# A hybrid decoder step: streams for block inverses and decode, norm and gate in two halves, shift state read first, one tile per feature block

## The chip, the cores and the metric

The kernel runs on one core of one Trainium2 chip. TensorE multiplies matrices, VectorE (DVE in the profile), ScalarE (ACT) and GpSimd (POOL) work on tiles, SyncE (SP) issues most transfers. The metric is the device time of one execution in microseconds (us); of several runs, the median.

## The reference

One inference step of two layers for 1040 prompt tokens (16 of them meta tokens) and 8 decode sequences of one token each, 1024 features, all in float32. Layer 0 is a Conformer convolution, layer 1 an RWKV-7 time mixing, each followed by an MLP with squared ReLU (1024 to 4096 to 1024). What matters here is the time mixing and what follows it:

```
xx = prev - h                      # prev: the row before; for decode, state_shift
r, k, v = (h + xx*mix_r) @ w_r, (h + xx*mix_k) @ w_k, (h + xx*mix_v) @ w_v
decay, a, g = small two-step projections of h + xx*mix
per token and head:  S = S*w + (S @ -kk) (kk*a)^T + v k^T ;  y = S r
y   = groupnorm_per_head(y) * gn_g + gn_b
out = (y + (sum r*k*r_k) * v) * g @ w_o
h   = h + out ;  h = h + relu(rmsnorm(h) @ w_in)^2 @ w_out ;  final rmsnorm
```

Outputs are the normalised rows, and the new convolution, shift and matrix states.

## The kernel before

**Stages.** Layer 0 runs over three token groups of about 350 (`G0`). Then the mixing stage runs over four groups of about 264 tokens (`G1`, `mixer_in(0)` to `mixer_in(3)`), and the last stage, the output projection and the second MLP, over three groups (`G2`): group 0 alone, then groups 1 and 2 together. Products of weights and activations in layer 0, in the output projection and in the MLPs are made of three passes: weights and activations are split into a high and a low part (`split`, `load_w`), and `mm3` (L185) multiplies high by high, low by high and high by low. The projections r, k, v of the mixing stage use one float32 product (`proj`).

**The recurrence in chunks.** The state update is done in 17 chunks of 64 tokens (chunk 0 holds the 16 meta tokens). A chunk needs the inverse of small triangular blocks of 32. `inverses(c, n)` (L1116) reads n chunks' blocks from DRAM (`ni`), does 30 steps of one multiplication and one addition on VectorE (L1127, L1128), and writes the result to DRAM (`d_p`). `front(c)` (L1142) loads a chunk's operands, multiplies them (`A`, L1168), and turns the inverse into `x32`; `chunk(c)` then computes gg, W, po, U, S and Y. In the kernel before, `front` begins with the inverses: for chunk 0 alone, and at chunks 1, 5, 9 and 13 for four chunks. They can begin once the mixing group that makes the blocks has run its `tail`, which is placed behind the two small projections (`p_g`, `p_wa`) of the next group.

**Order.** Within `tc.manual_schedule` TensorE executes in the order in which the program issues; that holds for the mixing stage, and for the output projection and MLP of group 0. The order on the other engines, and on TensorE elsewhere, is chosen by a planner from modelled times. The recurrence, the norm and gate and the decode step are Python generators that are advanced at marked points. In the mixing stage the point is `tick` (L1412): it adds 2.0 credits to the recurrence (none in group 0), which spends them by the numbers that it yields (`RW`, together 27.72 per chunk), and takes one step of norm and gate. A group has a tick before each r projection and two within each projection, 56 in groups 1 and 2, 40 in group 3. `step(c + 1)` takes one step of the next chunk's front without a charge, three times per chunk. In the MLP the point is `fill` (208 of them for group 0), and `filler` (L285) advances each stream in proportion to a total (`FA`, `NGA`).

**Norm and gate.** `norm_gate(i)` (L1362) handles 128 tokens in two halves of 512 features: it loads y, takes mean and variance per head, normalises, transposes on TensorE (`yn`, L1388), scales on ScalarE, adds the bonus `bv` and multiplies by the gate `gt`, and stores to `d_z`. Its steps follow each other. The square `sq` and the gated result `z` use one buffer (tag `eq`).

**Decode.** `decode_step` (L1320) updates the eight states on VectorE in 16 pieces. It comes first in the stream that then does norm and gate, and uses that stream's buffers (`ey`, `eq`).

**Other lines of the change.** `prepare(g)` (L781) loads a group's rows and makes `xx`; in the last group it also reads the shift state, transposes it, and writes the new one. `narrow_w` (L908) loads the first weights of the small projections in two halves. `mlp_in` (L263) makes the MLP's activations `m_h`, `m_l` and, first, the sum of squares by ones on TensorE (`st_m`, L231), whose result `rs` is needed only behind the first product (`r`, L327). `mixer_out` (L1443) loads z block by block (`zr`), splits it (`z_h`, `z_l`) and multiplies by the output weights (`ps_oo`). Memory comes from pools that are opened one behind the other; a tile of a new pool waits until the tile that lay there is done with.

Of the kernel before, what the change touches and what calls it, by code (L numbers as in the profile page):

```python
# [16 lines left out]
P = 128  # L17
# [31 lines left out]
def hybrid_step(tc, x_prompt, x_sample, state_conv, state_shift, state_wkv, meta_tokens,  # L49
# [10 lines left out]
    with ctx:  # L60
# [133 lines left out]
        def dense(w, act, n, name, fill=None):  # L194
            ps = bank(f"ps_{name}")
            for k in range(KT):
                mm3(ps[:, :n], (w[0][:, k, :], w[1][:, k, :]), (act[0][:, k, :n], act[1][:, k, :n]), k == 0, k == KT - 1)
                if fill and k == KT // 2 - 1:
                    fill()
            return ps  # L200

# [61 lines left out]
        def mlp_in(pl, hv, n, layer, name, sums):  # L263

            rs = rstd_of(mean_bcast(sums, n, name), n, 0, name, "rsm", 2)
            ah, al = new_act(pl, name, cur["wide"])
            for k in range(KT):
                g = vec("norm_mlp", layer * KT + k)
                nc.scalar.activation(ah[:, k, :n], hv[:, k, :], AF.Copy, scale=g)
                nc.vector.scalar_tensor_tensor(al[:, k, :n], hv[:, k, :], g, ah[:, k, :n].bitcast(F32),  # L270
                                               op0=ALU.mult, op1=ALU.subtract)
            return ah, al, rs
# [30 lines left out]
        def mlp(layer, groups, lag, eng_w, eng_h, fill=None, done=None):  # L303
# [15 lines left out]
            def inp(j, w, group):  # L319
# [440 lines left out]
        def open_ep(stack, bufs, tag):  # L760
            for name in ("ey", "ebv", "egt", "eq"):
                cur[name] = pool(stack, name + tag, bufs if name == "ey" else 1)
        open_ep(ld, 1, "d")
# [15 lines left out]
        prep, norm = {}, {}  # L779

        def prepare(g):  # L781
# [16 lines left out]
            if npr < n:  # L798
                sst = cur["raw"].tile([P, D], F32, name="sst", tag="raw")
                nc.scalar.dma_start(sst[:DEC, :], state_shift[0])  # L800
                pv = bank("pv", "x")
                for k in range(KT):
                    nc.tensor.transpose(pv[:, k * DEC:(k + 1) * DEC], sst[:DEC, k * P:(k + 1) * P], ident[:DEC, :DEC])
                sps = hnp.tile([P, KT, DEC], F32, name=nm("sps"), tag="sps")
                nc.scalar.copy(sps.rearrange("p k b -> p (k b)"), pv[:, :KT * DEC])
                nc.vector.tensor_sub(xx[:, :, npr:n], sps, hx[:, :, 1 + npr:1 + n])
                so = cur["raw"].tile([P, D], F32, name="so", tag="raw")
                for half in range(2):
                    pv = bank(f"pso{half}", "x")
                    for q in range(4):  # L810
                        nc.tensor.transpose(pv[:DEC + 1, q * P:(q + 1) * P], hx[:, half * 4 + q, npr:npr + DEC + 1], ident)
                    nc.scalar.copy(so[:DEC + 1, half * 512:(half + 1) * 512], pv[:DEC + 1, :])
                nc.scalar.dma_start(o_shift_prompt[0], so[0:1, :])
                nc.scalar.dma_start(o_shift_sample[0], so[1:DEC + 1, :])

# [7 lines left out]
            prep[g] = mix, hx, sps if npr < n else None  # L823
# [56 lines left out]
        def mixer_in(g, tick):  # L880
# [13 lines left out]
            mix, hx, sps = prep.pop(g)  # L894
# [13 lines left out]
            def narrow_w(i, name):  # L908

                out = []  # L910
                for hf in range(2):
                    raw = wide.tile([P, D], F32, name=nm(name, hf) + "_raw", tag="wide")
                    nc.sync.dma_start(blocks_of(raw), d_lr[i, :, hf * HK:(hf + 1) * HK].rearrange("p k s c -> p (k s) c"))
                    out.append(blocks_of(raw))
                return out

            def narrow(ws, name):

                ps = bank(nm("p", name))[:, :n]
                for k in range(KT):  # L920
                    w, j = ws[k // HK], k % HK * 2
# [104 lines left out]
            for p, rk2 in ahead_of(fetch):  # L1026
# [61 lines left out]
                late = finish(p, rk, ab, vv)  # L1088
                if g < 3:
# [15 lines left out]
        st = {"done": -1, "ready": -1, "credit": 0.0}  # L1105
# [10 lines left out]
        def inverses(c, n):  # L1116
# [16 lines left out]
            yield 1  # L1133

# [51 lines left out]
        def step(c):  # L1186

            if c < NCH and c <= st["ready"]:
# [5 lines left out]
        def chunk(c):  # L1194

            while c > st["ready"]:
# [111 lines left out]
        rec = ranked(RC, recurrence())  # L1308

# [10 lines left out]
        def decode_step():  # L1320

            with ExitStack() as s:
# [18 lines left out]
                rows = lambda t: t[:, :HV * HS].rearrange("p (v k) -> p v k", k=HS)  # L1341
                for hv in range(HS // HV):
                    vs = slice(hv * HV, (hv + 1) * HV)
                    S = rows(cur["ey"].tile([P, 4 * P], F32, name=f"Sdec{hv}", tag="ey"))
                    t4 = rows(cur["eq"].tile([P, 4 * P], F32, name=f"t4{hv}", tag="eq"))
# [14 lines left out]
                nc.scalar.dma_start(d_y[NP_TOK:].rearrange("b (h c) -> (b h) c", c=HS), yd)  # L1360

        def norm_gate(i):  # L1362

            lo, n = GN[i]
            KH, NH = KT // 2, KT
            for hf in range(2):
                ps_ = slice(hf * KH, (hf + 1) * KH)
                y, bv, gt, sq = (cur[tag].tile([P, KH * P], F32, name=f"{tag}{i}_{hf}", tag=tag) for tag in ("ey", "ebv", "egt", "eq"))
# [219 lines left out]
```

## Time and profile before

| | us |
|---|---|
| median of three runs (2882.78 to 2883.34) | 2883.28 |
| the profiled execution | 2880.81 |
| its span | 2878.8 |
| TensorE (PE) busy | 2674.6 |
| VectorE (DVE) busy | 1792.9 |
| GpSimd (POOL) busy | 1428.5 |
| ScalarE (ACT) busy | 1188.9 |

The mean granted clock of TensorE is 0.966 of full speed. In the profile the small projections `p_g` of the four mixing groups start at 1166, 1296, 1504 and 1723 us, the first output projection (`ps_oo`) at 1895, and the first matmul of the second output projection at 2298. Rows give time, engine, line of the kernel, instruction, written tile and read tiles; the brackets behind a row of the timeline give the idle time of the engine before it and what ended it.

### The profile page before, as it was taken

The page shows a single profiled execution, that of the slowest core. Times are in us where ns is not written, and L with a number is a line of the kernel's source. Part 1 is how long each engine was busy: PE and PEld are TensorE (multiplying, and loading weights), DVE is VectorE, ACT ScalarE, POOL GpSimd, SP SyncE. Part 2 cuts the span into 40 slices and gives each one's busy share as a digit, 9 for nine tenths or more (in the row PEclk, how much of TensorE's full clock was granted, in tenths as well). Part 3 has the DMA queues.
Part 4 walks back from the last instruction along what each step waited for, and adds up shares of the span by engine and source line. Part 5 has one row for each costly group of instructions (what it writes and reads, how often), then busy time and mean ns, then how long its engine had stood idle before and what let it go on. Part 6 is the DMA issues. An engine that isn't in the chain of part 4 may idle for free.

```text
span 2878.8 us, 51580 instructions
## 1 busy us (share of the span) xinstructions
PE 2674.6 (93%) x19594; PEld 2528.6 (88%) x19594; DVE 1792.9 (62%) x3618; ACT 1188.9 (41%) x2233; POOL 1428.5 (50%) x1983
## 2 busy tenths in 40 slices
PE   8999999999999898996988997968988999999998
PEld 7998999999999898885876876857888999999998
DVE  5999999995455544345656455469866554443444
ACT  5545444544354332332443553534444452222223
POOL 6677777987798773000001010156556783433432
PEclk9999999999999999998998999979999999999999
DMA  6663544454445643686776775685756542222221
GB/s 176 177 186 89 155 139 131 136 178 137 139 140 153 188 140 106 183 218 164 182 187 173 184 174 143 154 213 146 173 166 189 166 142 85 66 70 70 66 59 41
DMA packets 649654, 416.42 MB, mean 145 GB/s; under 512 B 126184, under 2 KB 600360, under 8 KB 649406
## 3 DMA queue, kind: packets, MB, share of 16 engines
q1 hardware_dynamic: 643164, 410.20, 50.6%
q10 hardware_dynamic: 6018, 2.89, 0.4%
q8 instruction: 155, 2.54, 0.4%
q14 instruction: 93, 0.76, 0.1%
q0 software_dynamic: 224, 0.03, 0.0%
HBM read 345.60 MB, written 68.37 MB: 144 GB/s over the span
## 4 chain that ended last, share of the span: by engine, by line
PE 74%; DVE 13%; DMA 6%; issue 2%; ACT 2%; POOL 1%; SPq 0%; ACTq 0%; DVEq 0%; POOLq 0%
PE out L187 8%; PE ps_in L189 7%; PE ps_in L188 7%; PE ps_in L187 7%; PE out L188 7%; PE out L189 7%; PE pk L845 3%; PE pv L845 3%; PE pr L845 3%; DVE cv L504 2%; PE A L1168 1%; PE ps_o L189 1%; PE ps_oo L187 1%; PE ps_o L188 1%; PE ps_o L187 1%
## 5 line engine op out<-in xcount | busy, mean ns | idle before, releaser
L162 POOL TENSOR_TENSOR wo_lo<-wo_raw,wo_hi 128x256 fp32r<-128x256 f32 x736 | 560.0, 793 | 291.5 <-ACT wo_hi L157 285.3
L162 POOL TENSOR_TENSOR wi_lo<-wi_raw,wi_hi 128x256 fp32r<-128x256 f32 x640 | 487.2, 792 | 297.3 <-ACT wi_hi L157 285.5
L187 PE MATMUL out<-hh,wo_hi 128*128 128x352 f32 (+2 forms) x1536 | 503.9, 328 | 22.0 <-DVE r L327 12.3
L340 DVE TENSOR_TENSOR h<-h,out 128x352 f32<-128x352 f32 (+2 forms) x768 | 387.2, 511 | 197.5 <-PE out L189 197.0
L189 PE MATMUL out<-hl,wo_hi 128*128 128x352 f32 (+2 forms) x1536 | 495.2, 325 | 7.4 <-DVE hl L141 7.4
L187 PE MATMUL ps_in<-m_h,wi_hi 128*128 128x352 f32 (+2 forms) x1536 | 497.4, 324 | 0.7 <-DVE h L340 0.7
L188 PE MATMUL out<-hh,wo_lo 128*128 128x352 f32 (+2 forms) x1536 | 497.6, 324 | 0.0
L189 PE MATMUL ps_in<-m_l,wi_hi 128*128 128x352 f32 (+2 forms) x1536 | 496.0, 323 | 0.0
L188 PE MATMUL ps_in<-m_h,wi_lo 128*128 128x352 f32 (+2 forms) x1536 | 494.6, 322 | 0.0
L504 DVE SCALAR_TENSOR_TENSOR cv<-u,wdw,cv 128x352 f32<-128x352 f32 (+2 forms) x720 | 377.2, 574 | 0.7
L157 ACT CAST wi_hi<-wi_raw 128x1024 fp32r<-128x1024 f32 x160 | 168.0, 1050 | 399.5 <-PE out L189 200.4
L157 ACT CAST wo_hi<-wo_raw 128x1024 fp32r<-128x1024 f32 x184 | 193.2, 1050 | 325.7 <-PE out L189 150.7
L187 PEld LDWEIGHTS out<-hh,wo_hi 128*128 128x128 f32 x1536 | 293.4, 191 | 27.9 <-DVE h L340 9.8
L189 PEld LDWEIGHTS out<-hl,wo_hi 128*128 128x128 f32 x1536 | 292.8, 191 | 9.4 <-DVE hl L141 9.2
L188 PEld LDWEIGHTS out<-hh,wo_lo 128*128 128x128 f32 x1536 | 293.5, 191 | 0.7
L187 PEld LDWEIGHTS ps_in<-m_h,wi_hi 128*128 128x128 f32 x1536 | 291.1, 190 | 2.4 <-issue 1.1
L188 PEld LDWEIGHTS ps_in<-m_h,wi_lo 128*128 128x128 f32 x1536 | 291.0, 189 | 1.0 <-issue 0.2
L189 PEld LDWEIGHTS ps_in<-m_l,wi_hi 128*128 128x128 f32 x1536 | 290.8, 189 | 0.6
L327 DVE SCALAR_TENSOR_TENSOR r<-ps_in,rs_m 128x352 f32<-128x352 f32 (+2 forms) x192 | 98.7, 516 | 233.6 <-PE ps_in L189 229.9
L141 DVE TENSOR_TENSOR hl<-s,hh 128x352 fp32r<-128x352 f32 (+2 forms) x192 | 145.3, 758 | 107.1 <-ACT hh L140 106.6
L329 ACT ACTIVATE s<-r 128x352 f32<-128x352 f32 (+2 forms) x192 | 93.8, 490 | 142.8 <-DVE r L327 142.7
L845 PE MATMUL pv<-mx,wv_raw 128*128 128x256 f32 (+2 forms) x512 | 125.7, 393 | 4.6 <-ACT rk L1029 4.6
(349 smaller groups left out, 4795.8 us busy)
## 6 DMA issues: line engine op xcount, KB each, us to landing
wi_raw<-in_w_mlp_in_dram SPq DMA_DIRECT2D x160, 512.0 KB
wo_raw<-in_w_mlp_out_dram SPq DMA_DIRECT2D x160, 512.0 KB
wk_raw<-in_rwkv_w_k_dram SPq DMA_DIRECT2D x32, 512.0 KB
wr_raw<-in_rwkv_w_r_dram SPq DMA_DIRECT2D x32, 512.0 KB
wv_raw<-in_rwkv_w_v_dram SPq DMA_DIRECT2D x32, 512.0 KB
d_ab<-ab SPq DMA_DIRECT2D x32, 512.0 KB
pg_raw<-in_conv_w_pw_dram SPq DMA_DIRECT2D x24, 512.0 KB
pa_raw<-in_conv_w_pw_dram SPq DMA_DIRECT2D x24, 512.0 KB
```

The source lines that it names most:

```text
L141: eng_lo.tensor_sub(lo, src, hi.bitcast(F32))
L157: nc.scalar.copy(hi[:, :a * b], raw[:, :a * b])
L162: eng_lo.tensor_sub(lo[:, cs], raw[:, cs], hi[:, cs].bitcast(F32))
L187: nc.tensor.matmul(ps, w[0], act[0], start=first, stop=False)
L188: nc.tensor.matmul(ps, w[1], act[0], start=False, stop=False)
L189: nc.tensor.matmul(ps, w[0], act[1], start=False, stop=last)
L327: nc.vector.scalar_tensor_tensor(r[:, :n], ps[:, :n], 0.0, rs[:, :n], op0=ALU.max, op1=ALU.mult)
L329: nc.scalar.activation(s[:, :n], r[:, :n], AF.Square)
L340: nc.vector.tensor_add(hv[:, 4 * i + m, :], hv[:, 4 * i + m, :], ps[:, :n])
L504: nc.vector.scalar_tensor_tensor(acc[m][:, :n], ug[:, m, j:j + n], wdw[:, m, j:j + 1], acc[m][:, :n], op0=ALU.mult, op1=ALU.add)
L845: nc.tensor.matmul(ps[:, :n], w[:, k, :], act[k], start=k == 0, stop=k == KT - 1)
L1168: nc.tensor.matmul(ps[:, i * 2 * P:(i + 1) * 2 * P], bk[:, j + i, :], xa[:, j + i].rearrange("p q x -> p (q x)"), start=True, stop=True)
```

## The change

- `inverses` are no longer part of `front`. `tail` puts them into a list, and each tick takes one step of the first of them (`invert`), before the recurrence is advanced. A chunk may begin when its inverses are through (`st["inv"]`). After the last group the list is drained.
- `decode_step` is a stream of its own in the fill points (total 82), with buffers of its own; the norm and gate of the tokens that hold the decode rows waits for it (`st["decoded"]`). The total of norm and gate becomes 180, `FA` 1.5 instead of 1.57.
- `norm_gate` takes a list of units; the second part of each half (transposes, scaling, bonus, gate, store) is issued behind the normalise step of the next half. Two buffers for y in the mixing stage.
- The shift state is loaded and transposed before the first group (`shift_in`); the new one is written in group 3 (`shift_out`).
- `narrow_w` loads four quarters into four buffers of half the size.
- The activations of the output projection and of layer 1's MLP are one tile per feature block (`new_acts`), and `mlp_in` of layer 1 gives a function that computes `rs` when it is first used.
- The pool of raw weights is opened once for the mixing and the last stage; in the last stage the activations' pool comes second; the squares of the sums use the tag `t2` instead of three buffers of their own; `mixp` has 24 buffers instead of 25.

```diff
         def dense(w, act, n, name, fill=None):
...
+        def new_acts(pl, name, nmax):
+            return [[pl.tile([P, nmax], F32R, name=f"{name}_{q}{k}", tag=f"act{q}{k}") for k in range(KT)] for q in "hl"]
...
-            rs = rstd_of(mean_bcast(sums, n, name), n, 0, name, "rsm", 2)
-            ah, al = new_act(pl, name, cur["wide"])
+            late = []
+
+            def rs():
+                if not late:
+                    late.append(rstd_of(mean_bcast(sums, n, name), n, 0, name, "rsm", 2))
+                return late[0]
+            ah, al = (new_acts if layer else new_act)(pl, name, cur["wide"])
+            if not layer:
+                rs()
...
-                    nc.vector.scalar_tensor_tensor(r[:, :n], ps[:, :n], 0.0, rs[:, :n], op0=ALU.max, op1=ALU.mult)
+                    nc.vector.scalar_tensor_tensor(r[:, :n], ps[:, :n], 0.0, rs()[:, :n], op0=ALU.max, op1=ALU.mult)
...
+        cur["raw"] = pool(lm, "wrawd", 5)
...
-        cur["raw"] = pool(ld, "wrawd", 5)
-        wide = pool(ld, "wided", 2)
-        mixp = pool(ld, "mixp", 25)
+        wide = pool(ld, "wided", 4)
+        mixp = pool(ld, "mixp", 24)
...
-                for hf in range(2):
-                    raw = wide.tile([P, D], F32, name=nm(name, hf) + "_raw", tag="wide")
+                for q in range(HK):
+                    raw = wide.tile([P, 4 * P], F32, name=nm(name, q) + "_raw", tag="wide")
...
-                st["ready"] = CHUNKS[g][0] + 3
+                for c, k in ([(0, 1)] if g == 0 else []) + [(ch0, ncg)]:
+                    invs.append(inverses(c, k))
...
+            st["inv"] = c + n - 1
...
-            if c == 0:
-                yield from inverses(0, 1)
-            if c % 4 == 1:
-                yield from inverses(c, 4)
...
+        def invert():
+            while invs:
+                wait = next(invs[0], None)
+                if wait is not None:
+                    return wait
+                invs.pop(0)
...
+            for i, hf in ((i, hf) for i in units for hf in range(2)):
+                while st["done"] < NEED[i] or (sum(GN[i]) > NP_TOK and not st["decoded"]):
+                    yield 1
+                lo, n = GN[i]
+                y = cur["ey"].tile([P, KH * P], F32, name=f"ey{i}_{hf}", tag="ey")
+                nc.sync.dma_start(y[:n], d_y[lo:lo + n, hf * KH * P:(hf + 1) * KH * P])
+                if behind:
+                    behind = load_rest(*behind)
+                yield 3
...
+                yield 2
+                if behind:
+                    second_half(*behind)
+                    yield 2.5
+                behind = i, hf, y
+            behind = load_rest(*behind)
+            yield 4
+            second_half(*behind)
+            yield 2.5
...
         def tick(g, slow):
+            invert()
             advance(PACE[g] * slow, NCH - 1)
             next(ng0, None)
...
-            open_weights(l1, 5, {"w": 5}, "f")
             open_tmp(l1, N2, "2", 3)
+            actp = pool(l1, "actp1", 1)
+            open_weights(l1, 0, {"w": 5}, "f")
             residp = pool(l1, "resid1", 1)
-            actp = pool(l1, "actp1", 1)
...
-            NGA, NGB, FA, FB = 262.15, 45.48, 1.57, 40
+            NGA, NGB, FA, FB = 180, 45.48, 1.5, 40
...
-                                ([decode_step(), norm_gates(GN_OF[1]), ng2], NGA))
+                                ([decode_step()], 82), ([norm_gates(GN_OF[1]), ng2], NGA))
```

More of the change, by code (lines that the diff above doesn't have):

```diff
@@ L779, in hybrid_step, with shift_in, shift_out @@
         prep, norm = {}, {}
+        sst = cur["raw"].tile([P, D], F32, name="sst", tag="raw")
+        nc.scalar.dma_start(sst[:DEC, :], state_shift[0])
+        sps = masks.tile([P, KT, DEC], F32, name="sps")
+        def shift_in():
+            pv = bank("pss", "x")
+            for k in range(KT):
+                nc.tensor.transpose(pv[:, k * DEC:(k + 1) * DEC], sst[:DEC, k * P:(k + 1) * P], ident[:DEC, :DEC])
+            nc.scalar.copy(sps.rearrange("p k b -> p (k b)"), pv[:, :KT * DEC])
+        def shift_out(hx, npr):
+            so = cur["raw"].tile([P, D], F32, name="so", tag="raw")
+            for half in range(2):
+                pv = bank(f"pso{half}")
+                for q in range(4):
+                    nc.tensor.transpose(pv[:DEC + 1, q * P:(q + 1) * P], hx[:, half * 4 + q, npr:npr + DEC + 1], ident)
+                nc.scalar.copy(so[:DEC + 1, half * 512:(half + 1) * 512], pv[:DEC + 1, :])
+            nc.scalar.dma_start(o_shift_prompt[0], so[0:1, :])
+            nc.scalar.dma_start(o_shift_sample[0], so[1:DEC + 1, :])
         def prepare(g):
@@ L821, in mix @@
                 return t[:, :n]
-            prep[g] = mix, hx, sps if npr < n else None
+            prep[g] = mix, hx
         def blocks_used():
@@ L1088, in mixer_in @@
                 late = finish(p, rk, ab, vv)
+                if g == 3 and p == 2:
+                    shift_out(hx, npr)
                 if g < 3:
@@ L1186, in step @@
         def step(c):
-            if c < NCH and c <= st["ready"]:
+            if c < NCH and c <= st["inv"]:
                 if c not in fronts:
@@ L1194, in chunk @@
         def chunk(c):
-            while c > st["ready"]:
+            while c > st["inv"]:
                 yield None
```

126 lines of the change are left out of this document (58 added, 68 removed).

## The prediction

> **What bounds the kernel now.** I read the page's busy shares first, then the list of who waited for whom on TensorE, then busy time by stretch, then TensorE's timeline around each wait, and last the chain of work that ended last.
>
> ```profile
> span 2878.8 us, 51580 instructions
> PE 2674.6 (93%) x19594; PEld 2528.6 (88%) x19594; DVE 1792.9 (62%) x3618; ACT 1188.9 (41%) x2233; POOL 1428.5 (50%) x1983
> ```
>
> TensorE is busy for 93% of the span, so the change can win only its idle time (about 204 us) and the slow-clock time that follows idle time. The change removes no matmul. So the question is which of TensorE's waits it removes. TensorE's waits, longest in total first (what waited, for whom, us in total, times, longest):
>
> ```profile
> PE gg L1206 <- DVE x L1182: 30.2, 2, 16.9
> PE yn L1388 <- DVE ey L1384: 25.0, 6, 7.3
> PE ps_oo L187 <- ACT z_h L140: 22.2, 2, 12.7
> ...
> PE yn L1388 <- issue: 9.1, 2, 5.2
> ...
> PE st_m L231 <- ACT sq L242: 7.3, 1, 7.3
> ...
> PE p_wa L922 <- DMA wa_raw<-d_lr: 6.5, 3, 5.7
> ...
> PE pv L803 <- DMA sst<-in_state_shift_dram: 1.7, 1, 1.7
> ```
>
> Every part of the change is aimed at one of these rows. Busy time by stretch (start:end and length; then PE, PEld, DVE, ACT, POOL; granted clock; DMA share; GB/s) shows where they lie and how full VectorE is there:
>
> ```profile
> 1542.00:1720.00 178.00, 159.89 (x1808) 133.16 (x1808) 104.00 (x240) 87.56 (x215) 14.39 (x29) 0.94 0.66 174
> ...
> 1880.00:1966.00 86.00, 52.91 (x508) 48.53 (x509) 64.16 (x127) 34.71 (x57) 44.62 (x60) 0.76 0.79 207
> 1966.00:2220.00 254.00, 221.74 (x2094) 211.57 (x2093) 193.10 (x391) 115.46 (x226) 150.82 (x182) 0.94 0.62 170
> 2400.00:2879.00 479.00, 469.50 (x2958) 468.32 (x2956) 207.32 (x389) 129.73 (x208) 170.44 (x229) 1.00 0.22 66
> ```
>
> The last 479 us have no waits and full clock: nothing to win there. From 1880 to 1966 TensorE is idle for 33 of 86 us; from 1966 to 2220 for 32 of 254.
>
> **What a wait costs beside itself.** TensorE's timeline (start, us, instruction, idle before it and its releaser) at three waits:
>
> ```profile
> 1308.55 1.22 PE L922 MATMUL p_wa<-hx,wa_raw 128*128 128x256 f32 x2 [5.65 <-DMA wa_raw<-d_lr]
> 1309.56 1.06 PE L923 MATMUL p_wa<-hx,wa_raw 128*128 128x256 f32 x2
> ...
> 1315.41 0.59 PE L923 MATMUL p_wa<-hx,wa_raw 128*128 128x256 f32 x2
> ...
> 1666.80 0.71 PE L1388 MATMUL yn<-ident,ey 72*128 72x72 f32 x4 [2.87 <-DVE ey L1384]
> 1667.30 1.16 PE L845 MATMUL pr<-mx,wr_raw 128*128 128x256 f32 x2
> ```
>
> After the 5.65 us wait a pair of passes takes 1.06 us, and some 6 us later 0.59. The pairs follow each other about 0.86 us apart instead of 0.43, so the wait costs some 2.5 to 3 us more. After only 2.87 us of idling a pair takes 1.16 us too. I charge 2.5 us for each wait of about 2.9 us or more. The Trainium skill, "TensorE: Matmul & The Clock Gate", section "Why this matters for your kernels", says to avoid idle gaps over about 3 us, since a window of idling brings back the half clock. The 2.87 us row says that a little less is enough; by the page's bound the sum below would win 2.5 us less (one gap fewer), 2822 or 2823.
>
> **The change part by part.**
>
> (1) Norm and gate in two halves, in the mixing stage. TensorE's order is written by hand there, so a transpose whose operand is late stops everything behind it. Its four waits:
>
> ```profile
> 1483.56 1.09 PE L1388 MATMUL yn<-ident,ey 128*128 128x128 f32 x4 [6.68 <-DVE ey L1384]
> ...
> 1575.62 1.12 PE L1388 MATMUL yn<-ident,ey 128*128 128x128 f32 x4 [7.33 <-DVE ey L1384]
> ...
> 1684.13 0.47 PE L1388 MATMUL yn<-ident,ey 72*128 72x72 f32 x4 [1.88 <-ACT uv L1254]
> ```
>
> With the 2.87 above that is 18.8 us. Before, a unit goes load, sums, normalise, transpose in four consecutive ticks. Now the transposes stand four ticks behind their normalise step, after the next half's load and sums; a tick is about 2 us of matmuls (14 ticks in 30 us, worked out below). So about 8 us of projection matmuls cover a wait of at most 7.3. Next late: the last half, which has one tick less of cover. If the cover is gone, all 18.8 us come back. I take 17 us of idling and three clock charges (7.5): 24 us. Bounds 0 and 29.
>
> (2) The same in the MLP stage. The yn waits of the list (25.0 + 9.1) and the 1.88 of ScalarE's just above, less 18.8, leave 17.2 us. The stream of norm and gate is now advanced by 180/208 of a unit per fill point (262.15/208 before, with the decode step in it), and the transposes stand 9.5 units, 11 points, behind normalise. I take 13 us and three charges: 20.5. Bounds 0 and 27 (all of it and four charges).
>
> (3) Start of the RWKV output projection.
>
> ```profile
> 1894.60 0.64 PE L187 MATMUL ps_oo<-z_h,wo_hi 128*128 128x328 f32 x1 [12.69 <-ACT z_h L140]
> ...
> 1898.70 0.64 PE L189 MATMUL ps_oo<-z_l,wo_hi 128*128 128x328 f32 x1 [3.18 <-DVE z_l L141]
> ...
> 1910.49 0.64 PE L187 MATMUL ps_oo<-z_h,wo_hi 128*128 128x328 f32 x1 [9.51 <-ACT z_h L140]
> ```
>
> 25.4 us. Before, z_h is one tile for all feature blocks, in a pool opened after the weights' and lying on memory that the last tail of the mixing stage still writes from; wo_raw comes from a new pool too. Now raw weights keep one pool through both stages, the activations' pool comes second, and z is 16 small tiles on memory that the last projection gives back. Next late are the sixteen casts and subtractions of z, of which TensorE needs one pair per block, and the eight zr loads through three buffers. I take 19 us and 3 of clock: 22. Bounds 0 and 30.
>
> (4) The sum of squares behind the first dense of the MLP.
>
> ```profile
> 1939.71 0.31 PE L188 MATMUL ps_oo<-z_h,wo_lo 128*128 128x328 f32 x1
> 1939.86 0.31 PE L189 MATMUL ps_oo<-z_l,wo_hi 128*128 128x328 f32 x1
> ...
> 1958.12 1.46 PE L231 MATMUL st_m<-sq,ones_d 128*128 128x328 f32 x2 [7.28 <-ACT sq L242]
> ```
>
> The 24 matmuls of the first dense (0.15 us from start to start in the first two rows, so some 4 us) go first, and m_h can be cast block by block as z's blocks come free, instead of waiting for the whole tile. I take 6 us and 2 of clock: 8. Bounds 0 and 10. Price on the other side: for the last two groups the sums wait in two of the three t2 buffers through a whole output projection, so the next group's squares start late; 0 to 10 us, I take 2.
>
> (5) Gate and decay weights in four quarters instead of two halves. The first quarter of wa comes free after four of g's 16 instruction pairs instead of eight, 1.7 us earlier, and TensorE needs a quarter, not a half. Of 6.5 us I take 4, with one clock charge 6.5. It doubles these loads (16 more issues over four groups) on SP's queue ahead of the projection weights, which are five buffers ahead; without that cover perhaps 2 us. Bounds -2 and 9.
>
> (6) The shift state read first: the 1.7 us of its row, and no clock charge; bounds 0 and 1.7. Its eight transposes now stand ahead of the first keys, its load issued in the stage before; the output transposes go to group 3.
>
> (7) Block inverses as a stream. This does not do what its place in the list promises. TensorE at the starts of groups 1 and 3 (first projection, then the gg that waits):
>
> ```profile
> 1320.01 3.62 PE L845 MATMUL pr<-mx,wr_raw 128*128 128x256 f32 x16
> ...
> 1349.05 1.46 PE L845 MATMUL pr<-mx,wr_raw 128*128 128x256 f32 x6
> 1367.41 1.06 PE L1206 MATMUL gg<-x,no 32*32 32x32 f32 x32 [16.91 <-DVE x L1182]
> ...
> 1742.46 3.72 PE L845 MATMUL pr<-mx,wr_raw 128*128 128x264 f32 x16
> ...
> 1786.97 1.07 PE L1206 MATMUL gg<-x,no 32*32 32x32 f32 x32 [13.33 <-DVE x L1182]
> ```
>
> and one product of a chunk in group 2:
>
> ```profile
> 1520.39 1.15 PE L1261 MATMUL S<-uv,bkt 128*64 128x64 f32 x32
> ```
>
> Counting credits (two per tick) through the code, gg of chunk 0 is issued at tick 14 of group 1 before, and at tick 14 after: the inverse takes nine ticks, the recurrence starts at the tenth, and its front costs 9.5 credits. The same count holds for chunk 9 in group 3. TensorE needs 30.5 us for these ticks (1320.01 to 1350.5), the inverse is ready 47.4 us after the first projection in group 1 and 44.5 in group 3. Both waits stay; I take 0. And a new one comes: before, the inverse for chunks 5 to 8 began inside chunk 4 and was charged to the recurrence, and no gg waited there. Now chunk 4 ends by tick 6 of group 2 and gg of chunk 5 also stands at tick 14. TensorE gets there after 30.5 us and some 5 us of chunk 4's last four products (each about the 1.15 of S), the inverse after about 46: 10 us, of which I take 9, with clock 11.5 lost. Bounds 0 and 19.5 (the wait of group 1 with its charge).
>
> (8) Decode as a stream of 82 units over all 208 points. Its last step comes at the last points, and the last unit of norm and gate waits for it, so three blocks of transposes are issued after the MLP's last matmul. The yn row of 1483.56 stands 9.5 us behind its load:
>
> ```profile
> 1474.08 0.34 SPq L1369 DMA_DIRECT2D ey<-d_y  x1
> ```
>
> Three such steps and a store are over 30 us, which the next output projection (8 denses of 4 us, some 30 us) mostly hides if the planner puts it ahead. I take 6 lost; bounds 0 and 36 (all of it, with two charges).
>
> **Sum**: 24 + 20.5 + 22 + 8 + 6.5 + 1.7 = 82.7 won; 11.5 + 6 + 2 = 19.5 lost; net 63.2. The profiled execution takes 2880.8 us (span 2878.8 and 2.0 around it): 2817.6. The median of the three runs, 2883.3, is 2.5 above it: 2820.
>
> **Rivals.**
> VectorE takes the waits' place in the MLP stage. It is at 193 of 254 us from 1966 to 2220 and 64 of 86 before that; with TensorE quicker the same work fills more. Then (2), (3) and (4), 50.5 us, come to nothing: 2820 + 50.5 = 2870. Against it: the decode step's VectorE work, bunched before, is spread out over the whole MLP; one of its lines:
>
> ```profile
> L1356 DVE TENSOR_TENSOR t<-Sdec,dq x16: 404/548/1165, 1945.3 to 2060.6; 128x256 f32<-128x256 f32 x16
> ```
>
> The inverses do come in time, because VectorE gets other work out of their way: both gg waits go (30 us and two charges) and (7) costs nothing. 2820 - 35 - 11.5 = 2773. Against it: the tick count.
>
> Slower: ScalarE, in order, stands at the norm step's square until the store of the earlier half has landed, as square and gated result share one buffer. The view of the tile ey says that ScalarE already idles for it:
>
> ```profile
>   DMA d_z<-ez: 22.8, 12
> ```
>
> That is 1.9 us each in 12 halves. The store itself takes longer, by the chain that ended last:
>
> ```profile
> 1582.78 4.16 DMA d_z<-ez
> ```
>
> If each of 18 halves now holds ScalarE, and through it the recurrence's PSUM banks and TensorE, for 2.3 us more (4.2 less 1.9), and (1) and (2) are gone with it, 38 won stand against 19.5 + 41: 2906. It decides from 1.0 us per half ((38.2 - 19.5)/18). Against it: square and store are as many ticks apart as before.
>
> No effect: wins and new waits cancel, 2883.
>
> **How the numbers follow.** About 0.2% (6 us) is what a measurement of this kernel can tell from no change. The forecast, 2820, with its own range of 2775 to 2850, has 0.53; VectorE in the way (2870) 0.20; inverses in time (2773) 0.05; no change 0.04; slower (2906, or the same mechanism smaller) 0.18. So faster 0.78, same 0.04, slower 0.18. The range runs from 2773 (all upper bounds of the wins and no losses, 107 us, give 2777) to 2884, and leaves out the slower case and little else.
>
> **What would show it.** Right: yn gone from the long rows of TensorE's waits; the three ps_oo waits together under 8 us; st_m under 2; gg waits of 13 to 17 us in groups 1 and 3 still there and a new one of about 10 in group 2; clock from 1880 to 1966 above 0.9. Wrong: gg waits gone or doubled; yn waits at the end of the first MLP group; ScalarE idle for d_z well over 23 us; new waits of `out` and `ps_in` for VectorE. What would upset the whole is the planner: it orders VectorE, ScalarE and the queue anew, and a transfer waiting at the queue's head would hold weights that nothing here shows late.

## The result

| | before | after |
|---|---|---|
| median of ten runs, us | 2883.31 (2882.24 to 2889.11) | 2872.62 (2870.14 to 2880.37) |
| span of the profiled execution, us | 2878.8 | 2869.4 |
| TensorE busy, us | 2674.6 | 2672.5 |
| VectorE busy, us | 1792.9 | 1799.4 |
| granted TensorE clock | 0.966 | 0.967 |

The ratio is 0.9962, with a 95% interval of 0.9952 to 0.9971. The change wins 10.7 us where 63 were forecast. The direction was right. The time lies in the wide range (2773 to 2884), but outside the 2775 to 2850 that the forecast's own mechanism was given, and five sixths of the gain are missing.

**Profile after.** The page's head, then the list of TensorE's waits (what waited, for whom, us in total, times, longest):

```profile
span 2869.4 us, 51630 instructions
PE 2672.5 (93%) x19594; PEld 2526.5 (88%) x19594; DVE 1799.4 (63%) x3618; ACT 1188.2 (41%) x2235; POOL 1433.1 (50%) x1983
```

```profile
PE gg L1227 <- DVE x L1203: 49.2, 4, 19.3
PE out L187 <- DVE h L355: 14.4, 8, 6.0
PE p_wa L943 <- DMA wa_raw<-d_lr: 9.8, 2, 5.7
...
PE pv L865 <- ACT rk L1050: 6.8, 4, 4.0
...
PE ps_oo L187 <- ACT wo_hi L157: 5.4, 1, 5.4
PE yn L1413 <- ACT uv L1275: 5.3, 3, 2.0
PE S L1282 <- ACT uv L1275: 4.8, 1, 4.8
PE S L1282 <- DVE nr L1197: 4.0, 1, 4.0
...
PE A L1189 <- ACT ez L1417: 3.8, 1, 3.8
```

Set beside the list of before, most of the aimed-at rows did what was forecast: 34.1 us of `yn` waits for VectorE and issue are gone (some 6 us in short ones remain). The `ps_oo` waits for z, 25.4 us, are gone, and one of 5.4 for the cast of the weights (`wo_hi`) stands there. `st_m` and the shift state's row are gone. Only `p_wa`, the aim of the quarters, waits longer (9.8 us instead of 6.5). In their place `gg` waits 19 us longer, `out` waits for `h` twice as long, and the recurrence's products S, U, Y and A wait 3 to 5 us at places that the list of before does not have. In all, TensorE's idle time (span less busy time) went only from 204.2 to 196.9 us.

The stages show where. The cuts are the starts of the first `p_g`, `ps_oo` and `ps_in` matmul of each group; the second number is TensorE's idle time in the stage, both in us, added up from the trace:

| stage | before | after |
|---|---|---|
| mixing group 0 | 129.4 (1.3) | 129.6 (1.7) |
| mixing group 1 | 208.6 (33.6) | 215.9 (32.5) |
| mixing group 2 | 218.8 (21.9) | 214.1 (28.4) |
| mixing group 3 | 171.4 (31.5) | 172.5 (29.6) |
| output projection, first group | 64.3 (20.0) | 59.8 (11.8) |
| MLP, first group | 339.0 (36.6) | 326.1 (30.6) |
| the rest | 580.9 (0.9) | 585.8 (4.4) |

By the prediction the mixing stage should have won 32.2 us (steps 1, 5 and 6) and lost 11.5 (step 7). It lost 4 (the four groups together). The output projection and the MLP's first group together won 17.4, where steps (2), (3) and (4) forecast 50.5. By these cuts the first `ps_oo` wait, 12.7 us before and 5.4 after, still belongs to group 3.

TensorE's timeline at the three `gg` waits of groups 1, 2 and 3 (start, us, instruction, idle before it and its releaser):

```profile
1367.36 1.06 PE L1227 MATMUL gg<-x,no 32*32 32x32 f32 x32 [19.27 <-DVE x L1203]
...
1590.32 1.07 PE L1227 MATMUL gg<-x,no 32*32 32x32 f32 x32 [14.77 <-DVE x L1203]
...
1795.13 1.06 PE L1227 MATMUL gg<-x,no 32*32 32x32 f32 x32 [13.52 <-DVE x L1203]
```

The waits of groups 1 and 3 stayed, and group 2 has the new one, as step (7) said. Its size is not as said. In group 2 the first projection, the load of the blocks, two stretches of the inverse's steps, and its end (the slowest steps come first):

```profile
1527.43 2.86 PE L865 MATMUL pr<-mx,wr_raw 128*128 128x256 f32 x12
```

```profile
1533.00 0.59 SPq L1146 DMA_DIRECT2D ni<-d_n  x1
```

```profile
1558.88 0.40 DVE L1151 TENSOR_TENSOR tt<-ni 128x234 f32<-128x234 f32 x1
...
1562.92 0.40 DVE L1151 TENSOR_TENSOR tt<-ni 128x238 f32<-128x238 f32 x1
...
1567.74 0.20 DVE L1441 RECIPROCAL ems<-ems 128x8 f32<-128x8 f32 x1 [1.95 <-ACT ems L1440]
1567.87 0.36 DVE L1151 TENSOR_TENSOR tt<-ni 128x240 f32<-128x240 f32 x1
...
1576.82 0.39 DVE L1151 TENSOR_TENSOR tt<-ni 128x220 f32<-128x220 f32 x1
1577.24 0.39 DVE L1152 TENSOR_TENSOR ni<-ni,tt 128x220 f32<-128x220 f32 x1
1577.66 0.38 DVE L1151 TENSOR_TENSOR tt<-ni 128x210 f32<-128x210 f32 x1
...
1589.73 0.45 DVE L1203 STREAM_TRANSPOSE x<-p 128x256 f32<-128x256 f32 x1 [5.48 <-DMA p<-d_p]
```

The load is issued 5.6 us after the first projection. The first 18 of the 30 steps of the inverse (one `tt`, one `ni` each) take 37.8 us, until TensorE has run out of work (1538.17 to 1575.98). The slowest of them are 4 to 5 us apart from start to start (1558.88, 1562.92, 1567.87). The last twelve take 8.3 us, the first of the rows shown 0.84 (1576.82 to 1577.66). Added up from the trace, the 30 steps take:

| inverse waited for in | steps, us | own busy time | VectorE's other work | VectorE idle |
|---|---|---|---|---|
| group 1 (chunk 0) | 30.3 | 19.0 | 9.1 | 2.2 |
| group 2 (chunks 5 to 8) | 46.1 | 21.2 | 18.2 | 6.7 |
| group 3 (chunks 9 to 12) | 31.9 | 19.7 | 10.3 | 1.9 |

In group 2 the recurrence's masks and the norm's halves stand between the steps: twice as much other work as in group 1, and some waits (1.95 us for ScalarE in the row of 1567.74). Behind the last step come 5.5 us of store and load through DRAM. So the inverse is ready 62.9 us after the first projection (1590.32 - 1527.43). The prediction had 46, from groups 1 and 3. TensorE is late as well: it comes to `gg` 48.1 us after the first projection (the row of 1590.32 less its 14.77 us), where the prediction had 35.5. The wait is the difference, 14.8 us instead of 10.

### The profile page after: what moved, and what is told of

Its sections match the earlier page's. It is cut to its first block, busy times and chain, and to the rows that moved or that the text cites. A ratio compares the mean times of both kernels' runs of the same rounds, so it can differ in the third digit from the quotient of the medians.

```text
span 2869.4 us, 51630 instructions
## 1 busy us (share of the span) xinstructions
PE 2672.5 (93%) x19594; PEld 2526.5 (88%) x19594; DVE 1799.4 (63%) x3618; ACT 1188.2 (41%) x2235; POOL 1433.1 (50%) x1983
## 4 chain that ended last, share of the span: by engine, by line
PE 72%; DVE 12%; DMA 6%; POOL 3%; issue 3%; ACT 3%; SPq 0%; DVEq 0%; ACTq 0%; POOLq 0%
PE out L187 7%; PE out L189 7%; PE out L188 7%; PE ps_in L187 7%; PE ps_in L189 7%; PE ps_in L188 7%; PE pk L865 4%; PE pv L865 3%; PE pr L865 3%; DVE cv L519 1%; POOL wo_lo L162 1%; DVE tt L1151 1%; POOL wi_lo L162 1%; DVE ni L1152 1%; PE A L1189 1%
```

## The experiments

The theory after the result (A in the expectations): the inverse stream costs more than was charged, and the rest of the change wins some 30 us or more. Against it stand, under further letters, that the gain of the halves or of the tiles and pools is given back in the next stage, or that VectorE's load takes it; each expectation says what it sets against what. Each run has its own runs of the kernel before on the same chip; ratios are to those.

**The inverses back in front of their chunks, all else as changed.**

```diff
-                for c, k in ([(0, 1)] if g == 0 else []) + [(ch0, ncg)]:
-                    invs.append(inverses(c, k))
+                st["inv"] = CHUNKS[g][0] + 3
...
-            st["inv"] = c + n - 1
...
+            if c == 0:
+                yield from inverses(0, 1)
+            if c % 4 == 1:
+                yield from inverses(c, 4)
```

> The changed kernel with the block inverses back in the front of chunks 0, 1, 5, 9 and 13; all other parts of the change stay. Theory A (the inverse stream eats the gain: it makes the gg wait of 14.8 us in group 2 and fills VectorE in the first output projection): the gg wait of group 2 goes, the two of 17 and 13 us in groups 1 and 3 stay, and the kernel takes 2845 to 2860 us. Theory B (in a fixed order the removed waits come back at other operands, whatever part is undone): 2866 to 2880 us.

Measured 2849.81 us, ratio 0.9862 (0.9847 to 0.9876). Moving the inverses back wins more than twice what the whole change won: 24.1 us by the profiled spans (2869.4 - 2845.3), 1.0% or 29 us by the ratios. Its `gg` row, and groups 1 and 2 by stretch, first in the changed kernel, then here (start:end and length; PE, PEld, DVE, ACT, POOL busy; clock; DMA share; GB/s):

```profile
PE gg L1229 <- DVE x L1205: 30.0, 2, 16.5
```

```profile
1295.10:1511.00 215.90, 183.39 (x1875) 154.10 (x1874) 129.41 (x327) 87.52 (x229) 17.44 (x33) 0.93 0.69 172
1511.00:1725.10 214.10, 185.73 (x1958) 155.90 (x1957) 118.87 (x272) 96.46 (x239) 18.28 (x33) 0.93 0.67 174
```

```profile
1294.60:1495.80 201.20, 173.19 (x1667) 146.24 (x1666) 123.23 (x317) 79.30 (x212) 13.97 (x29) 0.93 0.70 181
1495.80:1703.50 207.70, 190.94 (x2166) 160.64 (x2165) 123.84 (x282) 102.96 (x253) 21.45 (x37) 0.97 0.74 188
```

In both kernels the two groups together hold 3833 matmuls. They take 430.0 us with the stream and 408.9 without: 21.1 of the 24.1 us lie here. Of these, 17.5 are `gg` waits of these two groups (19.27 + 14.77 against 16.50). The stream let recurrence work come earlier (208 matmuls more in group 1), and most of its cost is that TensorE then waited for the inverse.

**The stream alone, in the kernel before.** The same edit the other way round: `invs`, `invert` and `st["inv"]` as in the change's diff, nothing else.

> The kernel before with one part of the change alone: the block inverses as a stream. Theory A: a gg wait of 10 to 15 us appears in group 2, the two others stay, and the kernel gets slower by 10 to 25 us: 2893 to 2908 us. Theory B: 2878 to 2888 us.

Measured 2908.97 against 2889.45 us, ratio 1.0068 (1.0053 to 1.0084): 19.5 us lost. The `gg` row shows four waits, as in the changed kernel:

```profile
PE gg L1204 <- DVE x L1180: 44.1, 4, 19.9
```

The new one, in group 2, is 8.9 us here, close to the 9 of step (7); the whole loss is larger than the 13.9 us by which the row grew. By stages, group 1 became 12.6 us longer and the output projection 12.3 (76.6); why the latter did is not shown.

**The stream kept, a chunk held back eight ticks.** The inverse is issued as in the change. The chunk may begin only eight ticks after the inverse's last step was issued, so TensorE has projections to do in the meantime.

```diff
-            st["inv"] = c + n - 1
+            due.append([c + n - 1, 8])
...
-        invs = []
+        invs, due = [], []
...
+            for e in due:
+                e[1] -= 1
+            while due and due[0][1] <= 0:
+                st["inv"] = due.pop(0)[0]
...
+            st["inv"] = NCH - 1
```

> The changed kernel, with a chunk allowed to begin eight ticks after the last step of its inverse was issued instead of at once, so that gg stands at tick 22 of a group instead of 14. Theory A: the three gg waits at group starts (19.3, 14.8 and 13.5 us) fall below 3 us each and, with their slow-clock time, 40 to 55 us are won: 2818 to 2833 us. Theory B: the time comes back elsewhere, above all in the MLP, which gets one more chunk: 2855 us or more.

Measured 2825.19 us, ratio 0.9781 (0.9765 to 0.9798), 1.8% better than the change as made, and better than the inverses in their old place:

```profile
PE gg L1227 <- DVE x L1203: 9.1, 2, 7.7
```

The last added line stands behind the drain of the last inverse. Of the waits at group starts, 7.7 us in group 1 remain. The wait was one of order. The code let TensorE reach `gg` when the inverse had been issued, not when it was done.

**Thirteen ticks** (with the decode step in the norm's stream, for which the run after next shows no measurable difference):

```diff
-            due.append([c + n - 1, 8])
+            due.append([c + n - 1, 13])
```

> The kernel with chunks eight ticks later and the decode step in the norm stream, with 13 ticks instead of eight. The one gg wait left at a group start (7.8 us in group 1) goes: 6 to 11 us faster, ratio 0.973 to 0.975. If the recurrence that is pushed further into the MLP costs as much there: ratio 0.976 to 0.980.

Measured 2830.56 us, ratio 0.9801 (0.9786 to 0.9815): not faster than eight. More of the recurrence now runs in the next stages: the mixing stage is 14.5 us shorter than with eight ticks (the run with the decode step in the norm's stream), but the output projection takes 69.4 us (56.0) and the MLP's first group 343.3 (334.4). New rows are among the longest:

```profile
PE ps_in L187 <- ACT m_h L284: 9.2, 1, 9.2
...
PE pdd L1361 <- ACT dst L1364: 7.5, 1, 7.5
```

**The last inverse in the fill points.** In the change it is drained after the mixing stage; VectorE does its steps during the output projection. Here, on top of the eight ticks, it is advanced in the fill points.

```diff
-            while invert():
-                pass
-            st["inv"] = NCH - 1
...
+                    invert()
-                    yield wait
+                    yield wait or 1.0
```

> The kernel of the run before last (chunks begin eight ticks after their inverse) with the inverse of the last four chunks advanced one step per step of the recurrence in the fill points of the MLP, instead of drained at the end of the mixing stage. If the drained inverse, 45 us on VectorE beside the first output projection, is what makes the waits of S, U and Y there: 8 to 15 us faster than with the drain, about 2812 to 2818 us against 2825. If VectorE's load there is not what counts: within 5 us of 2825.

Measured 2830.33 us, ratio 0.9807 (0.9791 to 0.9823), no better than 0.9781. But the run does not test what it was meant to. The last inverse did not move: its steps lie 2.3 to 54.5 us behind the first `ps_oo` matmul here (1848.10 to 1900.26, `ps_oo` at 1845.78), and 2.6 to 55.1 us behind it with the drain (1856.29 to 1908.80, `ps_oo` at 1853.71). The order on VectorE is the planner's, and it put them where they were. What the drain costs stays open.

**The decode step back at the head of the norm's stream**, again on top of the eight ticks:

```diff
-            NGA, NGB, FA, FB = 180, 45.48, 1.5, 40
+            NGA, NGB, FA, FB = 262.15, 45.48, 1.5, 40
...
-                                ([decode_step()], 82), ([norm_gates(GN_OF[1]), ng2], NGA))
+                                ([decode_step(), norm_gates(GN_OF[1]), ng2], NGA))
```

> The kernel in which chunks begin eight ticks later (2825 us), with the decode step back at the head of the norm and gate stream at the old total of 262.15, its own buffers kept. If the decode step as a stream of its own wins because it spreads VectorE's work: 8 to 20 us slower, 2833 to 2845 us. If it costs what the prediction's term (8) says, by the last unit of norm and gate behind the MLP: 0 to 6 us faster, 2819 to 2825 us.

Measured 2822.03 us, ratio 0.9772 (0.9756 to 0.9788). The last stage takes 581.2 us instead of 589.0, but the whole does not differ from 0.9781 by more than the intervals. It has the lowest ratio of all runs, and is faster than both kernels.

**Norm and gate in halves alone, in the kernel before** (`norm_gate(units)` of the change, two buffers `ey`, `mixp` 24):

```diff
-        mixp = pool(ld, "mixp", 25)
+        mixp = pool(ld, "mixp", 24)
...
-        open_ep(ld, 1, "d")
+        open_ep(ld, 2, "d")
...
-            return ranked(NG, chain.from_iterable(after(NEED[g], norm_gate(g)) for g in gs))
+            return ranked(NG, norm_gate(gs))
```

> The kernel before with one part of the change alone: norm and gate in two halves, two buffers for y in the mixing stage (24 buffers of mixp instead of 25 to make room). Theory A: terms (1) and (2) of the prediction hold by themselves, 30 to 45 us won: 2838 to 2853 us, yn gone from the long waits. Theory B: yn gone from the long waits, but other waits grow, and 2870 to 2883 us.

Measured 2859.24 us, ratio 0.989 (0.9874 to 0.9907): 30 us won. The `yn` waits fell from 37.4 us, all rows, to 7.7 (the longest is 4.5). TensorE's waits in all fell by only 20 us (195.5 to 175.3), and the profiled span by 19.3 (2878.8 - 2859.5). The waits of the output projection are all still there, as the other parts are not made:

```profile
PE gg L1206 <- DVE x L1182: 29.9, 2, 16.5
PE ps_oo L187 <- ACT z_h L140: 27.2, 3, 14.0
...
PE st_m L231 <- ACT sq L242: 6.8, 1, 6.8
```

**Tiles, pools and the late sum alone, in the kernel before.** `new_acts`, the raw weights' pool for both stages, the activations' pool second, `rs()` as a function, squares in `t2`; norm and gate as before.

```diff
-                z = new_act(actp, f"z{g}", cur["wide"])
+                z = new_acts(actp, f"z{g}", cur["wide"])
...
-            rs = rstd_of(mean_bcast(sums, n, name), n, 0, name, "rsm", 2)
+            def rs():
```

> The kernel before with one part of the change alone: one activation tile per feature block, the pools in the new order, the sum of squares behind the first dense. By the prediction's terms (3) and (4) less its 2 us: 28 us faster, 2853 to 2862 us. If other waits come up at the same place (U, S and the first dense for ScalarE and VectorE), which the earlier runs point to: 5 to 15 us faster, 2868 to 2878 us, with the ps_oo waits gone all the same.

Measured 2886.55 us, ratio 1.0002 (0.9991 to 1.0013): nothing, though the aimed-at waits for z and `st_m` are gone from its list:

```profile
PE yn L1403 <- DVE ey L1399: 28.7, 8, 7.3
PE yn L1403 <- issue: 12.3, 2, 8.0
...
PE ps_oo L187 <- ACT wo_hi L157: 6.4, 1, 6.4
```

The output projection became shorter by 9.1 us (55.2) and the MLP's first group longer by 14.2 (353.2). The `yn` waits for VectorE and issue grew from 34.1 to 41.0 us, half of what the MLP gave back.

**The same with the halves added** (the last two runs' edits together):

> The kernel before with two parts of the change: tiles per block with the pools and the late sum, and norm and gate in two halves. The halves alone took 1.1% off, the tiles alone nothing: they won 14 us up to the first MLP product and the MLP of group 0 gave 14 back, with longer yn waits. Theory C (the late operands of the fixed order, yn above all, give it back): with the halves in place the 14 us stay won, the ratio is 0.983 to 0.985 and the MLP stage of group 0 takes at most 328 us. Theory D (VectorE, which has the same work in less time, gives it back): that stage takes 333 us or more, and the ratio is 0.986 to 0.990.

Measured 2846.34 us, ratio 0.9854 (0.9837 to 0.987). Against the halves alone (0.989) the tiles and pools are now worth 10 us by the ratios and 15 by the spans (2859.5 - 2844.6). The MLP's first group takes 328.7 us. Both numbers lie just outside what theory C said, and outside D. So the same edit is worth nothing while `yn` in the MLP waits for its normalise step, and 10 to 15 us with the halves in place.

**The same without most of the decode arithmetic**, to see whether VectorE's load counts too:

```diff
+                nc.gpsimd.memset(yd, 0.0)
...
+                    if hv == 0:
                         nc.vector.tensor_mul(t4, S, overv(2))
...
```

> The run with tiles and halves, with the arithmetic of 15 of the 16 decode pieces left out (their state is loaded and stored unchanged, their output rows are zero), so that VectorE has some 60 us less to do in the MLP of group 0. Theory D: that stage becomes 8 us shorter or more than in the run with tiles and halves. Theory C: less than 4 us shorter.

Measured 2839.42 us, ratio 0.9828 (0.9813 to 0.9842). The MLP's first group goes from 328.7 to 318.8 us, and VectorE's busy time in it from 250.8 to 196.3. So VectorE's load there does count, some 10 us for nearly all of the decode step's arithmetic (this variant leaves out work that the step needs).

**The gate and decay weights in halves again, all else as changed:**

```diff
-        wide = pool(ld, "wided", 4)
+        wide = pool(ld, "wided", 2)
...
-                for q in range(HK):
-                    raw = wide.tile([P, 4 * P], F32, name=nm(name, q) + "_raw", tag="wide")
+                for hf in range(2):
+                    raw = wide.tile([P, D], F32, name=nm(name, hf) + "_raw", tag="wide")
```

> The changed kernel with the small projections' weights again loaded in halves into two buffers. By the prediction's term (5): 6.5 us slower, about 2879 us. If the wait for them is set by the time at which the queue issues them and by how long they take to land, and not by the buffer: within 3 us of 2872.6, and p_wa waits as long.

Measured 2878.96 us, ratio 0.997 (0.9958 to 0.9982), against 0.9962 of the change. The median is the one that was expected, but the kernel before was slower on this chip too (2888.44). By the ratios the quarters are worth some 2 us, by the `p_wa` waits the same (12.1 us here, 9.8 with the quarters), and the intervals overlap: no gain is shown.

**The quarters by ScalarE's queue:**

```diff
-                    nc.sync.dma_start(v, d_lr[i, :, 2 * q:2 * q + 2].rearrange("p k s c -> p (k s) c"))
+                    nc.scalar.dma_start(v, d_lr[i, :, 2 * q:2 * q + 2].rearrange("p k s c -> p (k s) c"))
```

> The changed kernel with the quarters of the small projections' weights issued from ScalarE's queue instead of SyncE's, where they stand behind the operand loads of the next chunk. If their place in that queue sets the wait: the p_wa waits of 5.7 and 4.1 us fall below 2 us each, 4 to 12 us faster, ratio 0.992 to 0.995. If it is the time that a quarter takes to land beside the other transfers (8 us from issue): the waits stay within 2 us of what they are and the ratio within 0.2% of 0.9962.

Measured 2875.89 us, ratio 0.9959 (0.9944 to 0.9974): no time won. The wait became shorter and another longer:

```profile
PE pv L865 <- ACT rk L1050: 9.5, 4, 5.7
...
PE p_wa L943 <- DMA wa_raw<-d_lr: 6.5, 3, 3.6
```

In the changed kernel the longest wait was 5.65 us, in group 1, where a quarter was issued behind the recurrence's loads and used 8.2 us later; SyncE's queue, then TensorE:

```profile
1298.79 0.86 SPq L1176 DMA_DIRECT2D bk<-d_ab  x1
1299.74 0.85 SPq L934 DMA_DIRECT2D wa_raw<-d_lr  x1
```

```profile
1307.90 1.22 PE L943 MATMUL p_wa<-hx,wa_raw 128*128 128x256 f32 x2 [5.65 <-DMA wa_raw<-d_lr]
```

The place in the queue is part of that wait. How much of the rest is the transfer and how much its neighbours stays open.

## Why the prediction was right in direction and wrong in size

The forecast was 63.2 us won, and 10.7 were measured: 52 us are missing. The runs divide them.

- Steps (1) to (4), less the 2 us of (4): 72.5 forecast. The kernel before with the halves, the tiles, the pools and the late sum has these alone and won 42.4 (2888.78 - 2846.34). Some 30 us are missing here.
- Step (7): 11.5 lost by the forecast, 24 to 29 measured. Some 12 to 18 us are missing here.
- Steps (5), (6) and (8) should have won 2.2 together. The change without the inverse stream won 39.6 (2889.45 - 2849.81), no more than the 42.4 of steps (1) to (4), so they won nothing that can be told from the noise.

By parts the runs add up too: halves -30 us (alone, in the kernel before), tiles, pools and late sum -10 (with the halves), inverse stream +29 (its removal, by the ratios), -11 together. By the profiled spans they are about -19, -15 and +24. That both sums come within 1 us of the measured 10.7 and 9.4 is in part luck, as each part is known to some 4 us at best.

**The step that failed first is the sum of the wins.** It added (1) to (4) as if each cured wait were won for good. The bounds of 0 allowed for lost cover at each place, and the first rival for the whole, but the sum did not. In the run without the inverse stream the output projection and the MLP's first group together won 14.5 us (54.6 and 334.2 against 64.3 and 339.0), where (2), (3) and (4) had 50.5 (12.7 us of (3)'s waits lie in group 3, which won 4.4); the mixing stage as a whole won 22.7 where (1), (5) and (6) had 32.2.

**Step (7), the inverse stream, is the other.** Its mechanism held: the waits of groups 1 and 3 stay, a new one comes in group 2, and the stream is a loss. Its size did not. It was charged 11.5 us with 19.5 as the upper bound. It measured 19.5 alone and 24 to 29 within the change. The new wait was put at 9 and is 14.77, the one of group 1 at 0 more and is 2.4 longer than before. "The inverse after about 46" was taken from groups 1 and 3; in group 2 VectorE has twice as much other work between the steps, and it took 62.9. TensorE's 35.5 us to `gg` were 48.1. Eight ticks of delay turn this step from the largest loss into a gain: 0.9781 against 0.9862 with the inverses in their old place.

**Steps (1) and (2), the halves, 24 + 20.5.** Measured together at 30 (2889.45 - 2859.24; 27 to 36 by the ratio's interval). The 30 us of `yn` waits did go (29.7 of them, run alone). A third came back as small waits in many places (`pfs` 5.4 us instead of 3.2, `ps_oo` for z 27.2 instead of 25.4, `out` for h 8.9 instead of 7.6). Of the six clock charges, 15 us, the profiled run shows nothing: its mean clock is 0.966, as before. Its other runs have 0.966 to 0.968, the kernel before on that chip 0.962 to 0.966.

**Steps (3) and (4), 22 + 8 less 2.** In their own place they are right in kind: `ps_oo` waits 5.4 us instead of 25.4 and `st_m` is gone, and the output projection is 9 to 10 us shorter than before in the tiles' own run and in the run without the inverse stream. But alone they are worth 0, as the MLP gives the time back, and with the halves 10 to 15. The prediction also forecast a clock above 0.9 from 1880 to 1966:

```profile
1880.00:1966.00 86.00, 63.73 (x637) 57.65 (x633) 68.50 (x135) 41.35 (x82) 50.49 (x65) 0.84 0.70 179
1966.00:2220.00 254.00, 226.67 (x2162) 216.59 (x2161) 203.50 (x410) 116.98 (x218) 163.13 (x196) 0.95 0.63 178
```

It is 0.84 (0.76 before). The recurrence's products, which stand in the same order, now wait where z was waited for:

```profile
1928.34 1.15 PE L1273 MATMUL U<-w,p 64*64 64x64 f32 x32 [3.42 <-ACT wi_hi L157]
1944.96 1.97 PE L1282 MATMUL S<-uv,bkt 128*64 128x64 f32 x32 [4.77 <-ACT uv L1275]
1950.00 1.98 PE L1289 MATMUL Y<-sv,xa 128*64 128x64 f32 x32 [3.07 <-DVE ni L1152]
```

After its 4.77 us the S product takes 1.97 us, where the row of 1520.39 in the prediction has 1.15. Behind the 3.42 us, `ps_oo` matmuls take 0.47 us (1930.19), and 0.31 from 1934.78 on. The Trainium skill, "TensorE: Matmul & The Clock Gate", section "Why this matters for your kernels", warns of idle gaps over about 3 us; the gaps of 3.42 and 4.77 us agree with it. The third tells nothing of its own, as the products before it were slow already.

**Step (5), the quarters, 6.5:** some 2 at most, and not clear of 0; the wait grew, from 6.5 to 9.8 us. The smaller pieces did not come earlier; their place in the queue set a part of that. **Step (6), 1.7:** the row of the shift state is gone; the part was not run on its own. **Step (8), 6 lost:** the three blocks of transposes do stand behind the MLP's last matmul (2282.9 to 2299.2), and the last stage is 4.9 us longer. Without the separate stream that time is back, but no difference of the whole could be measured.

**The rivals.** The first, VectorE in the waits' place, gives 2870, and the time is 2872.6. The number is a coincidence, as the rival takes step (7) at 11.5. Its mechanism holds in good part: (2), (3) and (4) came to 14.5 us of 50.5 without the inverse stream, and its sign is there, as `out` waits 7.0 us for VectorE's `h` in the MLP's first group (the longest 6.0), where no such row stood before. Of the cause, VectorE's load, some 10 us are shown: leaving out decode arithmetic wins them from the run with tiles and halves, whose VectorE is busy for 199.8 of the 254 us (203.50 in the changed kernel). The argument against the rival, that the decode work would be spread over the whole MLP, did not hold: the state's products run from 1990 to 2147 us, before from 1939 to 2061. Which other late operands took the rest stays open. Inverses in time: no, `gg` waits rose. Its price was about right, though: eight ticks of delay bring the inverses nearly in time and win 1.8%, some 52 us, where the rival had 46.5. ScalarE held by the store of `d_z`: in the changed kernel it idles for it 25.3 us against 22.8, only 2.5 us more, so no.

```profile
ACT eq L1437 <- DMA d_z<-ez: 25.3, 7, 6.9
```

## What to carry to other kernels

In an engine whose order is fixed, a late operand that is cured can hand its time to the next late one: price the cures together, in the order of the waits, and not as a sum. Where a long chain on another engine feeds that order, gate the consumer by when the chain will be done, not by when it was issued, and take the chain's length from the stage in which it will run, with that stage's other work between its steps. Look for the delay on both sides: here eight ticks were right, none cost 1.8%, and thirteen moved the work into the next stage.

## What the runs showed that was not expected

The same 60 small VectorE instructions take 30.3 us in group 1 and 46.1 in group 2. Of the 15.8 us between them, 9.1 are other VectorE work between the steps, 4.5 are VectorE's own waits there, and 2.2 are longer instructions. So the time of a chain on a shared engine was set by what stood between its steps, above all by the neighbours' work. And an edit that removes 26 us of TensorE's waits by the list (25.4 to 6.4 of `ps_oo`, 7.3 to none of `st_m`) can measure 1.0002.
